# A dense block followed by sixteen streamed experts: the raw weights' pool is moved, and the first expert loads are put in another order

## The chip, the cores and the metric

One core of a Trainium2 chip runs the whole program. The metric is the device time of one execution in microseconds (us); what counts is the median over the runs. TensorE is called PE, VectorE DVE, ScalarE ACT, GpSimd POOL, and SyncE SP; SP issues most of the transfers.

## The reference, cut to what matters

A 512 x 1024 activation passes two mixer layers and then a second block: dense projections, three mixers, an output projection, a router, and a mixture of 16 experts in which each expert takes the 64 tokens that score highest for it.

```python
def second_block(...):
    ...
    mixed = jnp.concatenate([rms_norm_2(y_hy, ...), rms_norm_2(y_na, ...), rms_norm_2(y_pool, ...)], axis=-1)
    x = x + mixed @ w_out[i]
    x = x + expert_choice_moe(rms_norm_2(x, norm2_g[i]), w_router[i], w_gate[i], w_up[i], w_down[i])
    return rms_norm_2(x, final_g)

def expert_choice_moe(h, w_router, w_gate, w_up, w_down):
    cap = EC_CAPACITY * L // N_EXPERTS                    # 64 tokens
    aff = jax.nn.softmax(h @ w_router, axis=-1)
    gate, idx = lax.top_k(aff.transpose(0, 2, 1), cap)
    xs = jax.vmap(lambda hb, ib: hb[ib])(h, idx)
    a = jnp.einsum('becd,edf->becf', xs, w_gate)          # each expert: 3 matrices of 1024 x 2048, float32
    b = jnp.einsum('becd,edf->becf', xs, w_up)
    y = jnp.einsum('becf,efd->becd', jax.nn.silu(a) * b, w_down)
    ...
```

The weights of the experts are 16 x 3 x 8 MB = 402.7 MB of float32, and each byte is used once.

## The kernel before, in words

**Two stages.** The dense stage (both mixer layers, the second block's mixers and its output projection) runs first, out of pools that `build` opens one on top of the other in SBUF: `np` (norms and sums), `wp` (the dense weights), `xp` (the operands `xhi` and `xlo`, two buffers of 16 KB per partition each), and above these a pool that changes from mixer to mixer. A dense weight arrives raw (`wraw`, two buffers of 4 KB) and is split by ACT and DVE into `whi` and `wlo` (three buffers each); `group` multiplies them. The last four groups are the output projection: two that read the operand MA, one that reads MB, and one that reads `mn`. MA lies in an `xhi` buffer, MB in an `xlo` buffer, and `mn` in the other `xhi` buffer. In these four groups a PE row `acc<-xhi,wlo` is one of MA, `acc<-xlo,wlo` one of MB, and `acc<-mn,wlo` one of `mn`.

**The expert stage.** When the dense pools close, one pool of `moe_body` takes their room. An expert's weights come in 12 loads of 128 x 4096 float32 (2,097,152 bytes): four parts of the gate matrix (`mg`) and four of the up matrix (`mu`), in turns, then four of the down matrix (`md`); 192 loads in all. They land in nine places of 16 KB per partition, `w0` to `w8`, and for the first expert also in `ZH` and in the room of the activations `H` (called "t" in the code). `wtile` hands the places out: first in the order of the list `FIRST`, then round and round. Every load stands on SP's queue, in program order, by `load` and `preload`; SP issues one only after the waits of that load are over. A load's waits are those for whatever used the bytes of its place last.

**Where the places lie.** In KB from the start of a partition, by the built programs (the change moves only the dense side of this table):

| place | KB | dense tiles there, before | dense tiles there, after the change |
|---|---|---|---|
| ZH | 42.9 to 58.9 | norm temporaries, two `whi` | the same |
| w0 | 74.9 to 90.9 | `wraw`, half of the `mn` buffer | the `mn` buffer |
| w1 | 90.9 to 106.9 | half of `mn`, half of MA | MA |
| w2 | 106.9 to 122.9 | half of MA, half of MB | MB |
| w3 | 122.9 to 138.9 | half of MB, half of the other `xlo` | the other `xlo`, last read by the projections `qk0`, `qk1` |
| w4 | 138.9 to 154.9 | half of the other `xlo`, `YN` | `wraw`, `YN` |
| w5 to w8 | 154.9 to 218.9 | tiles of the mixers | the same |

**Between the stages** stands the router: PE computes the logits (`lg`) and the sums of squares (`nrm`), ACT copies the logits and takes the root, PE turns the logits (`lgT`), DVE and ACT make the softmax (`aff`), and `resid` transposes the activations (`xt`, copied to `res`). `rank` counts for each token of an expert how many score higher, and `gather` builds the expert's input. `idle` fills PE with matmuls whose result nobody reads.

**An expert.** `up` multiplies the gathered input with the `mg` and `mu` parts (64 matmuls each), `down` the result with the `md` parts (64); beside this `scatter` adds the expert before into the sum.

Of the kernel before, what the change touches and what calls it, by code (L numbers as in the profile page):

```python
# [19 lines left out]
S = 512  # L20
D = 1024
# [180 lines left out]
class Kern:  # L202
# [69 lines left out]
        if name in self.dbg:  # L272
            self.nc.gpsimd.dma_start(out=self.dbg[name], in_=ap)

    IDLE = 12, 2, 13


    WBUF = 3
# [16 lines left out]
    def fetch(self, w=None):  # L295
        if self.pos == len(self.seq):
            return
        nc = self.nc
        n, i, src = self.seq[self.pos]
        self.pos += 1  # L300
        if w is None:
            w = self.wp.tile([128, 2, 512], F32, name="wraw", bufs=2)
            (nc.gpsimd if n.startswith("wo") else nc.sync).dma_start(out=w, in_=src)
        hi = self.wp.tile([128, 2, 512], F32R, name="whi", bufs=self.WBUF)
        lo = self.wp.tile([128, 2, 512], F32R, name="wlo", bufs=self.WBUF)
        with self.tc.high_priority(1000):
# [110 lines left out]
    def pp_proj(self, l):  # L417

        nc = self.nc
        P = tuple(self.big.tile([128, 2, 512], F32R, name=n, bufs=1) for n in ("phi", "plo"))  # L420
        praw = self.wp.tile([128, 2, 512], F32, name="praw", tag="wraw", bufs=2)
        nc.scalar.dma_start(out=praw, in_=self.I["pT"][l])
        for k in range(2):
            self.split_x(P, k, praw[:, k, :])
        self.pp = self.big.tile([128, 8, 512], F32, name="pp", bufs=1)
        for half in range(2):
            wh, wl = self.take(f"pp{l}", half)
            for j in range(4):
                a = self.acc()
                c = slice(j * 128, j * 128 + 128)  # L430
                for k in range(2):
                    self.mm3(a, wh[:, k, c], wl[:, k, c], P[0][:, k, :], P[1][:, k, :], k == 0, k == 1)
                nc.scalar.activation(self.pp[:, half * 4 + j, :], a, AF.Copy)
# [35 lines left out]

    def X2(self):  # L470
        return tuple(self.xp.tile([128, 8, 512], F32R, name=n, bufs=2) for n in ("xhi", "xlo"))

    def open_dense(self):
        tc, ctx = self.tc, self.ctx
        self.np = ctx.enter_context(tc.tile_pool(name="np", bufs=1))
        self.wp = ctx.enter_context(tc.tile_pool(name="wp", bufs=1))
        self.xp = ctx.enter_context(tc.tile_pool(name="xp", bufs=1))

    def first(self, names):

# [908 lines left out]
    def mixout(self, M):  # L1389
# [23 lines left out]
            return t  # L1413

        def summed(t, first, last):
            for i in range(4):
                nc.tensor.matmul(nrm[:, i:i + 1], t[:, i * 128:i * 128 + 128], self.ones[:, :1], start=first and i == 0,
                                 stop=last and i == 3, skip_group_check=True)

        for g in range(2):  # L1420
            self.group(MA, f"wo{g}", "T", ev(g, False), steps=(3, 0))
# [17 lines left out]
        def ev1(j, a):  # L1439
            b = 4 + j  # L1440
            ev(1, False)(j, a)
            if b < 6:
                nc.gpsimd.tensor_add(sq, sq, square(b))
            else:
                S[b] = square(b)
            if b < 7:
                return lambda: self.logits(lg, b)

            def f():
                self.logits(lg, 7)  # L1450
                summed(sq, True, False)
                nc.vector.tensor_add(S[6], S[6], S[7])
                summed(S[6], False, True)
            return f

        self.group(M, "wo1", "T", ev1, (first4,), steps=(1, 2), apart=True)
# [9 lines left out]
    PARTS = 0, 2, 1, 3  # L1466


    FIRST = "w8", "w7", "w6", "w5", "w4", "w2", "w3", "ZH", "w0", "w1", "t"

    def moe_body(self, R, out, mp):
        nc, I = self.nc, self.I
# [10 lines left out]
        def wtile(keep=False):  # L1483

            n = (places or ring).pop(0)
            if n not in ring and n[0] == "w" and not keep:
                ring.append(n)
            if n == "t":
                return self.H.rearrange("p a c -> p (a c)")
            t = tile_(n)  # L1490
            if n == "ZH":
                early["ZH"] = t
            return t

        def load(e, i):


            n, i = SEQ[i]
            W[e, n, i] = w = wtile()
            src = I[n]  # L1500
            if e == 15 and i == (3 if n == "md" else self.PARTS[-1]):

                m = 1024 if n == "md" else 2048
                for k in range(0, 4096, m):
                    early["last"] = nc.sync.dma_start(out=w[:, k:k + m], in_=bass.AP(tensor=src.tensor, ap=[[4096, 128], [1, m]],
                                                      offset=src.offset + (e * 4 + i) * 128 * 4096 + k))
                return
            nc.sync.dma_start(out=w, in_=bass.AP(tensor=src.tensor, ap=[[4096, 128], [1, 4096]],
                                                 offset=src.offset + (e * 4 + i) * 128 * 4096))

        def preload(e, k0, k1):
            for i in range(k0, k1):
# [2 lines left out]
        def junk(name="junk"):  # L1515
# [1 line left out]


        tile_ = Tiles(mp, ss=(128, 3, 4), xt=(128, 8, 64, 2), oh=(128, 4, 64, 2), ZH=(128, 4096, 1), res=(128, 4, 1024, 1),
                      **{f"w{i}": (128, 4096, 1) for i in range(self.WB)}, rtok=(128, 4, 1), rs=(128, 4, 1), aff=(128, 4, 16, 1),  # L1520
                      mx=(128, 4, 1), cnt=(128, 3, 4, 2), rank=(128, 4, 3), fin=(128, 4, 4, 1), at=(128, 4, 2, 1), ai=(128, 1, 1), fl=(128, 4, 1))
        res = tile_("res")
        preload(0, 0, len(self.FIRST) - 1)
        lt = junk("lt")
        nc.scalar.activation(lt, lg, AF.Copy)
        r, mx, rs = tile_("rtok"), tile_("mx"), tile_("rs")
        nc.scalar.activation(rs, nrm[:, :4], AF.Sqrt, bias=self.eps, scale=1.0 / D)
        warm = tile_("ss")
        nc.scalar.activation(warm[:, 0:1], rs[:, 0:1], AF.Exp, scale=-1.0)
        V.reciprocal(r, rs)  # L1530
        aff = tile_("aff")
        p = self.tp("lgT")
        for i in range(4):
            routed = nc.tensor.matmul(p[:, i * 16:i * 16 + 16], lt[:, i * 128:i * 128 + 128], self.sel, start=i == 0, stop=i == 3,
                                      skip_group_check=True)
        p = p[:, :64].rearrange("p (i e) -> p i e", i=4)
        V.tensor_reduce(mx, p, AX.X, OP.max)
        V.tensor_sub(aff, p, mx[:, :, None].to_broadcast([128, 4, 16]))
# [77 lines left out]
        def up(e):  # L1616
# [5 lines left out]
            for at, (i, (n, A)) in enumerate(itertools.product(self.PARTS, (("mg", G), ("mu", U)))):  # L1622
                w = W.pop((e, n, i))
                for k in range(2):
                    for b in range(2):
                        for t in range(2):
                            c = k * 2048 + t * 1024 + b * 512
                            mm = nc.tensor.matmul(A[b][t * 64:t * 64 + 64, :], xt[:, 2 * i + k, :], w[:, c:c + 512],  # L1628
                                                  start=at < 2 and k == 0, stop=at > 5 and k == 1, skip_group_check=True)
                with self.tc.issue_after(mm.ins):  # L1630

                    if e and first <= at < first + 4:
                        scatter(e - 1, at - first)
# [103 lines left out]
        def resid(i):  # L1737
            for hf in range(2):
                q = self.acc("xt")
                for k in range(4):  # L1740
                    nc.tensor.transpose(q[:, k * 128:k * 128 + 128], h[:, hf * 4 + k, i * 128:i * 128 + 128], self.ident)
                nc.scalar.activation(res[:, i, hf * 512:hf * 512 + 512], q, AF.Copy)

        with self.tc.issue_after(routed.ins), self.tc.issue_after(ex.ins):
            resid(0)
            i = self.idle(self.IDLE[1])
        with self.tc.issue_after(i.ins):
            i = rank(0)
        with self.tc.issue_after(i.ins):
            for i in range(1, 4):  # L1750
                resid(i)
            self.idle(self.IDLE[2])
        gather(0)
        preload(0, len(self.FIRST) - 1, len(self.FIRST))
        total = None
        for e in range(15):
            preload(e, len(self.FIRST) if e == 0 else 0, NSEQ)
# [39 lines left out]
def build(ctx, tc, I, out, dbg=None):  # L1797
# [3 lines left out]
    def whole(fast):  # L1801
        with ExitStack() as es:
            K.np = es.enter_context(tc.tile_pool(name="np", bufs=1))
            K.wp = es.enter_context(tc.tile_pool(name="wp", bufs=1))
            K.xp = es.enter_context(tc.tile_pool(name="xp", bufs=1))
            X, sq = K.start(S_FOX + S_T0 + S_REC + S_T1 + S_SEC)
            A = K.fox(X, sq)
            K.h = K.H
# [31 lines left out]
```

## Time and profile before

| | us |
|---|---|
| median of 3 runs (1849.95 to 1851.24) | 1851.19 |
| the profiled execution | 1849.2 |
| its span, first to last instruction | 1847.0 |
| PE busy | 1792.5 |
| DVE busy | 839.7 |
| ACT busy | 495.7 |

The span has 2.2 us less than the profiled execution, which lie around it. PE is busy in 97% of the span, but the end of a matmul is modelled, so this share alone does not say that PE is at its limit. The transfers are half idle in the first half of the span, and from about the middle on they run at one rate without a break.

### The profile page before, as it was taken

Reading aid. Unit: us, or ns where it says so; the run is one execution under the profiler, and the core shown is the slowest. Engines: PE = TensorE matmul, PEld = TensorE weight load, DVE = VectorE, ACT = ScalarE, POOL = GpSimd, SP = SyncE. Lnnn points to the kernel's source line nnn. Section 1 sums busy time; section 2 is a strip of 40 time slices with the busy share of each in tenths; the row PEclk is TensorE's granted clock in tenths of the full one; section 3 lists DMA queues with packets and bytes.
Section 4 is the critical chain, followed back from the end, with each engine's and each line's share of the span. In section 5 each row is a group of like instructions: output and inputs, shape, how many; then the busy total and the mean of one; then the engine's idle time right before and its main releaser. Section 6 shows DMA issues by size and latency. Waiting matters only on the chain.

```text
span 1847.0 us, 21691 instructions
## 1 busy us (share of the span) xinstructions
PE 1792.5 (97%) x8654; PEld 1024.1 (55%) x8654; DVE 839.7 (45%) x1939; ACT 495.7 (27%) x863; POOL 21.8 (1%) x35
## 2 busy tenths in 40 slices
PE   9999999999999999999999999999999999999997
PEld 6767677888888888876743333333333333333332
DVE  6564767774644684678532223332223321333222
ACT  6453644463433464237401000000000000000011
POOL 0000000000000000000100000000000000000000
PEclk9999999999999999999999999999999999999999
DMA  5322233232221226434799999999999999999997
GB/s 168 114 81 86 75 118 128 101 99 95 65 80 57 96 88 219 132 117 172 286 403 403 421 426 428 427 428 427 428 427 428 427 427 428 428 427 429 427 427 323
DMA packets 57993, 497.18 MB, mean 269 GB/s; under 512 B 7017, under 2 KB 8169, under 8 KB 32667
## 3 DMA queue, kind: packets, MB, share of 16 engines
q1 hardware_dynamic: 48420, 470.46, 62.8%
q10 hardware_dynamic: 7592, 18.70, 3.1%
q0 software_dynamic: 1872, 6.55, 1.1%
q8 instruction: 70, 1.15, 0.2%
q14 instruction: 39, 0.32, 0.1%
HBM read 491.20 MB, written 4.49 MB: 268 GB/s over the span
## 4 chain that ended last, share of the span: by engine, by line
PE 75%; DMA 17%; DVE 5%; ACT 1%; issue 1%; ACTq 0%; POOLq 0%; SPq 0%; DVEq 0%
DMA w<-mu 11%; PE y L1675 11%; PE acc L339 11%; PE acc L340 11%; PE acc L341 10%; PE u L1628 8%; PE g L1628 7%; PE gx L1580 3%; PE st L1734 2%; DMA w<-mg 2%; DMA w<-md 2%; DMA wraw<-wg 1%; PE hT L1662 1%; PE pt L639 1%; PE sc L335 1%
## 5 line engine op out<-in xcount | busy, mean ns | idle before, releaser
L339 PE MATMUL acc<-xhi,whi 128*128 128x512 f32 x800 | 317.5, 399 | 0.9 <-ACT xhi L325 0.8
L341 PE MATMUL acc<-xhi,wlo 128*128 128x512 f32 x800 | 313.8, 393 | 0.0
L340 PE MATMUL acc<-xlo,whi 128*128 128x512 f32 x784 | 307.6, 392 | 0.2 <-DVE xlo L326 0.2
L1735 DVE TENSOR_TENSOR H<-H,st 128x512 f32<-128x512 f32 x120 | 78.1, 683 | 489.1 <-PE st L1734 489.1
L1628 PE MATMUL g<-w,xt 128*64 128x512 f32 x1024 | 260.2, 595 | 10.7 <-DMA w<-mg 10.6
L1628 PE MATMUL u<-w,xt 128*64 128x512 f32 x1008 | 248.0, 596 | 7.3 <-DMA w<-mu 6.9
L308 DVE TENSOR_TENSOR wlo<-wraw,whi 128x1024 fp32r<-128x1024 f32 x127 | 155.1, 1222 | 185.7 <-ACT whi L307 167.9
L1675 PE MATMUL y<-w,ZH 128*64 128x512 f32 x1008 | 237.0, 595 | 0.6 <-DMA w<-md 0.6
L307 ACT ACTIVATE whi<-wraw 128x1024 fp32r<-128x1024 f32 x127 | 134.3, 1057 | 214.1 <-PE acc L340 135.5
L339 PEld LDWEIGHTS acc<-xhi,whi 128*128 128x128 f32 x800 | 150.5, 188 | 37.8 <-issue 3.6
L1628 PEld LDWEIGHTS g<-w,xt 128*64 128x64 f32 x1024 | 79.5, 137 | 163.5 <-issue 135.6
L341 PEld LDWEIGHTS acc<-xhi,wlo 128*128 128x128 f32 x800 | 150.3, 188 | 30.9 <-issue 0.7
L340 PEld LDWEIGHTS acc<-xlo,whi 128*128 128x128 f32 x784 | 147.4, 188 | 32.2 <-issue 3.1
L1628 PEld LDWEIGHTS u<-w,xt 128*64 128x64 f32 x1008 | 76.3, 137 | 148.0 <-issue 126.7
L1675 PEld LDWEIGHTS y<-w,ZH 128*64 128x64 f32 x1008 | 73.9, 137 | 140.0 <-issue 136.6
L1648 ACT ACTIVATE gs<-g 128x512 f32<-128x512 f32 x32 | 19.1, 597 | 402.6 <-PE g L1628 386.3
L1580 PE MATMUL gx<-res,oh 128*64 128x256 f32 x512 | 62.3, 385 | 10.8 <-DVE H L1735 10.8
L1734 PE MATMUL st<-ZH 64*128 64x512 f32 x240 | 67.7, 641 | 0.0
L1612 ACT ACTIVATE ZH<-ogT 128x512 f32<-128x512 f32 x15 | 9.0, 597 | 207.1 <-PE ogT L1610 207.1
L339 PE MATMUL acc<-whi,xhi 128*128 128x512 f32 x160 | 64.3, 403 | 0.0
L341 PE MATMUL acc<-whi,xlo 128*128 128x512 f32 x160 | 62.9, 393 | 0.0
L340 PE MATMUL acc<-wlo,xhi 128*128 128x512 f32 x160 | 62.9, 393 | 0.0
(528 smaller groups left out, 1896.6 us busy)
## 6 DMA issues: line engine op xcount, KB each, us to landing
w<-mg SPq DMA_DIRECT2D x63, 2048.0 KB, 32.2
w<-mu SPq DMA_DIRECT2D x62, 2048.0 KB, 31.2
w<-md SPq DMA_DIRECT2D x62, 2048.0 KB, 34.7
wraw<-wg SPq DMA_DIRECT2D x115, 512.0 KB, 3.5
cb<-cd ACTq DMA_DIRECT2D x16, 256.0 KB, 3.5
wraw<-wg POOLq DMA_DIRECT2D x8, 512.0 KB, 3.8
nab<-nab ACTq DMA_DIRECT2D x12, 256.0 KB, 2.7
H<-xT SPq DMA_DIRECT2D x8, 256.0 KB, 5.5
```

The lines of the kernel that those rows point to most:

```text
L307: self.last = nc.scalar.activation(hi, w, AF.Copy)
L308: nc.vector.tensor_sub(lo, w, hi.bitcast(F32))
L335: mm(*a, skip_group_check=True, **k)
L339: mm(out, wh, xh, start=start, stop=False)
L340: mm(out, wh, xl, start=False, stop=False)
L341: mm(out, wl, xh, start=False, stop=stop)
L1580: nc.tensor.matmul(Q[w][t * 64:t * 64 + 64, :256], oh[:, i, :], rv[:, i, t, w], start=i == 0, stop=i == 3, skip_group_check=True)
L1628: mm = nc.tensor.matmul(A[b][t * 64:t * 64 + 64, :], xt[:, 2 * i + k, :], w[:, c:c + 512], start=at < 2 and k == 0, stop=at > 5 and k == 1 ...
L1648: nc.scalar.activation(g, G[b], AF.Silu)
L1675: nc.tensor.matmul(Y[t * 64:t * 64 + 64, :], hT[:, i % 2 * 4 + k, i // 2, :], w[:, k, t * 512:t * 512 + 512], start=kk == 0 and e < 15, st ...
L1734: nc.tensor.matmul(q, OHT[e][sl, i * 128:i * 128 + 128], YY[e][sl, :], start=True, stop=True)
L1735: V.tensor_add(total[:, i, t * 512:t * 512 + 512], total[:, i, t * 512:t * 512 + 512], q)
```

## The change

- The raw dense weights leave `wp` for a pool of their own, `wr`, which is opened above `xp`. The operand buffers thereby come to lie 8 KB lower, each of them on exactly one place (table above).
- `FIRST`, the order in which the places are handed out, and `ORDER`, the order in which the first ten loads are issued, are new: the first load goes to `w2`. The twelfth load, the last `md` part of the first expert, goes into `w2` again, in two halves, and it and what follows are now recorded after the first part of the first expert's matmuls.
- In the router the sums of squares are made with `ones` as the other operand (12 matmuls of 32 x 128 in place of 8 of 128 x 1; a sum on DVE goes away), the root is taken over 128 x 128 and turned by PE afterwards, the copy of the logits is shared by DVE and ACT, two idle matmuls stand earlier, half of the residual's transposes stand ahead of `rank`, and the last run of idle matmuls has 9 in place of 13.

```diff
-    IDLE = 12, 2, 13
+    IDLE = 12, 2, 9
...
-            w = self.wp.tile([128, 2, 512], F32, name="wraw", bufs=2)
+            w = self.wr_.tile([128, 2, 512], F32, name="wraw", bufs=2)
...
         def summed(t, first, last):
             for i in range(4):
-                nc.tensor.matmul(nrm[:, i:i + 1], t[:, i * 128:i * 128 + 128], self.ones[:, :1], start=first and i == 0,
-                                 stop=last and i == 3, skip_group_check=True)
+                m = nc.tensor.matmul(nrm[32 * i:32 * i + 32, :128], self.ones[:, :32], t[:, i * 128:i * 128 + 128], start=first,
+                                     stop=last, skip_group_check=True)
+            return m
...
-                nc.vector.tensor_add(S[6], S[6], S[7])
-                summed(S[6], False, True)
+                summed(S[6], False, False)
+                m = summed(S[7], False, True)
+                with self.tc.issue_after(m.ins):
+                    self.idle(self.IDLE[1])
...
-    FIRST = "w8", "w7", "w6", "w5", "w4", "w2", "w3", "ZH", "w0", "w1", "t"
+    FIRST = "w2", "w8", "w7", "w6", "w5", "w1", "w3", "w4", "ZH", "w0", "t"
+
+    ORDER = 0, 1, 2, 3, 4, 5, 6, 8, 7, 9
...
+            if early.get(n):
+                t, early[n] = early[n], None
+                return t
             t = tile_(n)
+            if n == self.FIRST[0] and n not in early:
+                early[n] = t
...
+                m = 2048 if (e, i, n) == (0, len(self.FIRST) - 8, "md") else 4096
+            for k in range(0, 4096, m):
+                early["last"] = nc.sync.dma_start(out=w[:, k:k + m], in_=bass.AP(tensor=src.tensor, ap=[[4096, 128], [1, m]],
+                                                  offset=src.offset + (e * 4 + i) * 128 * 4096 + k))
...
-        preload(0, 0, len(self.FIRST) - 1)
-        lt = junk("lt")
-        nc.scalar.activation(lt, lg, AF.Copy)
+        for i in self.ORDER:
+            load(0, i)
+        lt, rt = junk("lt"), junk("rt")
+        V.tensor_copy(lt[:, :256], lg[:, :256])
+        half = nc.scalar.activation(lt[:, 256:], lg[:, 256:], AF.Copy)
...
+            if i == 3:
+                nc.tensor.transpose(q[:, :128], rt[:, :128], self.ident)
...
+                if e + at == 0:
+                    preload(0, len(self.FIRST), NSEQ)
...
             resid(0)
-            i = self.idle(self.IDLE[1])
+            i = resid(1)
...
             K.xp = es.enter_context(tc.tile_pool(name="xp", bufs=1))
+
+            K.wr_ = es.enter_context(tc.tile_pool(name="wr", bufs=1))
```

SP's queue where the dense stage's last weight load is past, before (place, source, shape, and the engines whose progress the row itself waits for; a wait that an earlier row has made is not repeated):

```order
L1508 DMA w8_7435<-mg 128x4096 [waits DMAHW0_49,DMAHW1_49,DVE_49,PE_49]
L1508 DMA w7_7434<-mu 128x4096 [waits DMAHW1_49,DVE_49,PE_49]
L1508 DMA w6_7433<-mg 128x4096 [waits DMAHW4_49,DMAHW5_49,DMAHW3_49,DMAHW6_49,DMAHW2_49,DMAHW7_49,DVE_49,PE_49]
L1508 DMA w5_7432<-mu 128x4096 [waits PE_49,DVE_49,Activation_49,Pool_49]
L1508 DMA w4_7431<-mg 128x4096 [waits DVE_49]
L1508 DMA w2_7429<-mu 128x4096 [waits PE_49]
L1508 DMA w3_7430<-mg 128x4096
```

The same rows of SP's queue in the changed program:

```order
L1515 DMA w2_7439<-mg 128x4096 [waits DMAHW0_49,DVE_49,PE_49]
L1515 DMA w8_7445<-mu 128x4096 [waits DMAHW1_49]
L1515 DMA w7_7444<-mg 128x4096 [waits DMAHW2_49]
L1515 DMA w6_7443<-mu 128x4096 [waits DMAHW6_49,DMAHW5_49,DMAHW7_49,DMAHW4_49,DMAHW3_49]
L1515 DMA w5_7442<-mg 128x4096 [waits Pool_49]
L1515 DMA w1_7438<-mu 128x4096
L1515 DMA w3_7440<-mg 128x4096
L1515 DMA w4_7441<-md 128x4096 [waits DMASW4_49,DMASW3_49,DMASW5_49,DMASW2_49,DMASW6_49,DMASW1_49,DMASW7_49,DMASW0_49,DVE_49]
```

The load into `w2` has moved from the sixth row to the first, and its wait for PE with it. That wait is for the same matmul in both programs: the last one that reads MB. None of the seven rows behind it waits for PE on its own account any more, since the first row's wait is later in PE's order than any of theirs.

PE's router before, from the last logits to the first expert's ranking (`bc` is in `rank`):

```order
L1387 MATMUL lg<-H,wr 32x512 x4
L1417 MATMUL nrm<-ones,sqx_7095 128x1 x4
L1417 MATMUL nrm<-ones,sqx 128x1 x4
L1534 MATMUL lgT<-sel,lt 128x16 x4
L1741 MATMUL xt<-ident,H 128x128 x8
L268 LDWEIGHTS identb
L268 MATMUL idle<-identb 128x512
...
L1550 MATMUL bc<-ident,aff 128x128 x4
L1741 MATMUL xt<-ident,H 128x128 x24
```

The same stretch of PE's queue in the changed program:

```order
L1381 MATMUL lg<-H,wr 32x512 x4
L1412 MATMUL nrm<-sqx_7098,ones 32x128 x4
L1412 MATMUL nrm<-sqx,ones 32x128 x8
L268 LDWEIGHTS identb
L268 MATMUL idle<-identb 128x512
...
L1545 MATMUL lgT<-sel,lt 128x16 x4
L1755 MATMUL xt<-ident,H 128x128
L1544 MATMUL rootT<-ident,rt 128x128
L1755 MATMUL xt<-ident,H 128x128 x15
L1562 MATMUL bc<-ident,aff 128x128 x4
L1755 MATMUL xt<-ident,H 128x128 x16
```

The two idle matmuls have moved ahead of `lgT`, eight of the residual's transposes have moved ahead of `bc`, and the transpose of the root is new. Everything on PE ahead of this stretch stands in the same order in both programs.

## Rows read from the trace of the kernel before

**Rows 1.** The page's head, and its forty slices of the transfers.
```profile
span 1847.0 us, 21691 instructions
...
DMA  5322233232221226434799999999999999999997
GB/s 168 114 81 86 75 118 128 101 99 95 65 80 57 96 88 219 132 117 172 286 403 403 421 426 428 427 428 427 428 427 428 427 427 428 428 427 429 427 427 323
```
**Rows 2.** Windows: stretch, length, busy PE PEld DVE ACT POOL, PEclk, DMA, GB/s.
```profile
823.00:901.00 78.00, 77.22 (x462) 57.11 (x462) 58.17 (x173) 48.78 (x112) 3.16 (x6) 1.00 0.54 197
901.00:1100.00 199.00, 196.15 (x975) 81.61 (x976) 59.99 (x193) 24.14 (x38) 6.45 (x5) 0.99 0.97 407
1100.00:1350.00 250.00, 244.40 (x1170) 87.15 (x1166) 76.10 (x230) 10.75 (x18) 0.00 (x0) 1.00 1.01 427
1350.00:1800.00 450.00, 423.07 (x1998) 150.75 (x1996) 120.40 (x352) 23.62 (x40) 0.00 (x0) 1.00 1.01 427
```
**Rows 3.** Waits of PE, 1350 to 1847 us: us in total, times, longest.
```profile
PE g L1628 <- DMA w<-mg: 10.6, 11, 1.3
PE u L1628 <- DMA w<-mu: 6.9, 8, 1.2
...
PE y L1675 <- DMA w<-md: 0.6, 1, 0.6
```
**Rows 4.** Chain that ended last: ends of experts 0 and 2, expert 1's last part.
```profile
981.80 0.42 PE y L1675
...
1010.32 3.58 PE u L1628 x16
...
1092.71 0.42 PE y L1675
```
**Rows 5.** Timeline of SP, 820 to 936 us: start, length of the issue, operation.
```profile
823.97 0.33 SPq L1508 DMA_DIRECT2D w<-mg  x1
855.04 0.33 SPq L1508 DMA_DIRECT2D w<-mu  x1
869.16 0.33 SPq L1508 DMA_DIRECT2D w<-mg  x1
877.71 0.33 SPq L1508 DMA_DIRECT2D w<-mu  x1
895.09 0.33 SPq L1508 DMA_DIRECT2D w<-mg  x1
901.03 0.33 SPq L1508 DMA_DIRECT2D w<-mu  x1
```
**Rows 6.** Waits of SP, 820 to 1000 us: us in total, times, longest.
```profile
SPq L1508 <- PE acc L341: 5.6, 1, 5.6
```
**Rows 7.** Transfers issued 890 to 898 us: KB, us from issue to landing.
```profile
w<-mg SPq DMA_DIRECT2D x1, 2048.0 KB, 7.8
```
**Rows 8.** Timeline of PE, 840 to 912 us, single rows.
```profile
845.98 0.40 PE L340 MATMUL acc<-xlo,whi 128*128 128x512 f32 x1
...
889.73 0.39 PE L341 MATMUL acc<-xhi,wlo 128*128 128x512 f32 x1
...
900.61 0.39 PE L341 MATMUL acc<-xlo,wlo 128*128 128x512 f32 x1
900.84 0.39 PE L339 MATMUL acc<-mn,whi 128*128 128x512 f32 x1
```
**Rows 9.** Timeline of PE in the router, 914 to 936 us, three rows.
```profile
914.90 1.95 PE L1417 MATMUL nrm<-ones,sqx 128*128 128x1 f32 x16
...
923.65 2.97 PE L268 MATMUL idle<-identb 128*128 128x512 bf16 x13
...
930.70 1.02 PE L1628 MATMUL g<-w,xt 128*64 128x512 f32 x2
```
**Rows 10.** Windows, the ten us in which PE's clock is lowest.
```profile
910.00:920.00 10.00, 10.00 (x56) 7.31 (x55) 4.50 (x15) 5.72 (x11) 2.58 (x2) 0.87 0.83 329
```
**Rows 11.** Timeline of PE at the end of the span, the last two `md` parts.
```profile
1829.68 7.09 PE L1675 MATMUL y<-w,ZH 128*64 128x512 f32 x32 [0.58 <-DMA w<-md]
```

More of the change, by code (lines that the diff above doesn't have):

```diff
@@ L420, in pp_proj @@
         P = tuple(self.big.tile([128, 2, 512], F32R, name=n, bufs=1) for n in ("phi", "plo"))
-        praw = self.wp.tile([128, 2, 512], F32, name="praw", tag="wraw", bufs=2)
+        praw = self.wr_.tile([128, 2, 512], F32, name="praw", tag="wraw", bufs=2)
         nc.scalar.dma_start(out=praw, in_=self.I["pT"][l])
@@ L471, in X2 @@
         return tuple(self.xp.tile([128, 8, 512], F32R, name=n, bufs=2) for n in ("xhi", "xlo"))
[L473 to L477, printed above, removed]
     def first(self, names):
@@ L1503, in load @@
                 m = 1024 if n == "md" else 2048
[L1504 to L1509, printed above, removed]
+            else:
+                m = 2048 if (e, i, n) == (0, len(self.FIRST) - 8, "md") else 4096
+            for k in range(0, 4096, m):
+                early["last"] = nc.sync.dma_start(out=w[:, k:k + m], in_=bass.AP(tensor=src.tensor, ap=[[4096, 128], [1, m]],
+                                                  offset=src.offset + (e * 4 + i) * 128 * 4096 + k))
         def preload(e, k0, k1):
@@ L1519, in moe_body @@
         tile_ = Tiles(mp, ss=(128, 3, 4), xt=(128, 8, 64, 2), oh=(128, 4, 64, 2), ZH=(128, 4096, 1), res=(128, 4, 1024, 1),
-                      **{f"w{i}": (128, 4096, 1) for i in range(self.WB)}, rtok=(128, 4, 1), rs=(128, 4, 1), aff=(128, 4, 16, 1),
+                      **{f"w{i}": (128, 4096, 1) for i in range(self.WB)}, rtok=(128, 4, 1), aff=(128, 4, 16, 1),
                       mx=(128, 4, 1), cnt=(128, 3, 4, 2), rank=(128, 4, 3), fin=(128, 4, 4, 1), at=(128, 4, 2, 1), ai=(128, 1, 1), fl=(128, 4, 1))
         res = tile_("res")
-        preload(0, 0, len(self.FIRST) - 1)
-        lt = junk("lt")
-        nc.scalar.activation(lt, lg, AF.Copy)
[L1526 to L1530, printed above, removed]
+        for i in self.ORDER:
[3 more added lines that the diff above has]
+        half = nc.scalar.activation(lt[:, 256:], lg[:, 256:], AF.Copy)
+        r, mx = tile_("rtok"), tile_("mx")
+        with self.tc.issue_after(half.ins):
+            nc.scalar.activation(rt[:, :128], nrm[:, :128], AF.Sqrt, bias=self.eps, scale=1.0 / D)
+            warm = tile_("ss")
+            nc.scalar.activation(warm[:, 0:1], rt[:, 0:1], AF.Exp, scale=-1.0)
         aff = tile_("aff")
-        p = self.tp("lgT")
+        p, q = self.tp("lgT"), self.av("rootT")
         for i in range(4):
+            if i == 3:
+                nc.tensor.transpose(q[:, :128], rt[:, :128], self.ident)
             routed = nc.tensor.matmul(p[:, i * 16:i * 16 + 16], lt[:, i * 128:i * 128 + 128], self.sel, start=i == 0, stop=i == 3,
                                       skip_group_check=True)
+        V.reciprocal(r, q[:, 0:128:32])
         p = p[:, :64].rearrange("p (i e) -> p i e", i=4)
@@ L1740, in resid @@
                 for k in range(4):
-                    nc.tensor.transpose(q[:, k * 128:k * 128 + 128], h[:, hf * 4 + k, i * 128:i * 128 + 128], self.ident)
+                    t = nc.tensor.transpose(q[:, k * 128:k * 128 + 128], h[:, hf * 4 + k, i * 128:i * 128 + 128], self.ident)
                 nc.scalar.activation(res[:, i, hf * 512:hf * 512 + 512], q, AF.Copy)
+            return t
         with self.tc.issue_after(routed.ins), self.tc.issue_after(ex.ins):
             resid(0)
-            i = self.idle(self.IDLE[1])
+            i = resid(1)
         with self.tc.issue_after(i.ins):
@@ L1749, in moe_body @@
         with self.tc.issue_after(i.ins):
-            for i in range(1, 4):
+            for i in range(2, 4):
                 resid(i)
@@ L1756, in moe_body @@
         for e in range(15):
-            preload(e, len(self.FIRST) if e == 0 else 0, NSEQ)
+            if e:
+                preload(e, 0, NSEQ)
             if e == 13:
```

## The prediction

> **What bounds the kernel now.** I read the forty slices of the page first. From the twentieth slice on the transfers are busy in every slice and move 403 to 429 GB/s, while in the slices ahead they are mostly idle [rows 1]. The table by stages says the same with sharper ends: 427 GB/s and a full DMA share from 1100 to 1800 us [rows 2]. One load is 2.097152 MB, so at 427 GB/s it takes 2.097152 / 0.427 = 4.911 us, and an expert of twelve loads takes 58.9 us. PE alone is a little quicker: from the end of expert 0 to the end of expert 2 the chain counts 1092.71 - 981.80 = 110.9 us, 55.5 us for an expert [rows 4]. So PE, which begins with a stock of loads, gains 3.5 us on the transfers with each expert until the stock is gone. The waits of PE show where that is: none is named for a weight between 1100 and 1350 us (that view has only waits for DVE), and after 1350 us there are 11 waits for `mg` and 8 for `mu` [rows 3]. The last `md` matmuls start on the arrival of their weights too, after a wait of 0.58 us [rows 11]. From there to the end nothing of the change is found. Hence the stream of 192 loads sets the end: **what moves the end is when the stream starts and how much it idles before it is full**, and a microsecond gained by PE in the router is worth nothing by itself.
>
> **The start of the stream.** Five loads are issued before 901 us, one by one, as the places come free: 823.97, 855.04, 869.16, 877.71, 895.09 [rows 5]. The fifth lands 7.8 us after its issue [rows 7], at 902.9 us. The sixth, into `w2`, is issued at 901.03 [rows 5] after a wait of 5.6 us for a PE matmul of line 341 [rows 6]. It is the last that reads MB: it starts at 900.61 and the next row already reads `mn` [rows 8].
>
> **The changed order on SP.** In the changed program the load into `w2` stands first on SP's queue, and it waits for that same matmul, since `w2` now lies on MB alone. PE's order ahead of it is unchanged and PE is busy in 77.22 of the 78 us before it [rows 2], so it cannot come noticeably earlier; I take 901.03 us again. SP issues in order. The loads into `w8`, `w7`, `w6` and `w5`, whose places are free at 824 to 878 us as before, stand behind the waiting row, and so do those into `w1` (MA, last read at 889.73 [rows 8]) and `w3`. Who waits for that is the stream: the transfers do nothing for the experts before 901 us.
>
> What this costs, counted at the fifth load. Before it lands at 902.9. Now the first load lands at 901.03 + 7.8 = 908.8 and the fifth four loads later, at 908.8 + 4 x 4.911 = 928.5. The stream is behind by **25.6 us**.
>
> **What comes back.** Before, the stream is not full after 901 us: the stretch to 1100 us moves 407 GB/s in place of 427 [rows 2], which is 199 x (427 - 407) / 427 = 9.3 us of idle transfers, lost where a load waits for its place. Now eight loads are free to go at 901 us, and they alone keep the transfers busy to 901.03 + 2.9 + 8 x 4.911 = 943 us (the 2.9 is what the single load's 7.8 has beyond 4.911). `ZH` waits for the last of the sums of squares and `w0` for the last `mn` matmul; both are over when PE adds those sums up, from 914.90 us [rows 9]. The first load that needs anything of expert 0 is the twelfth, the halves of `w2`. Its turn comes at 908.8 + 10 x 4.911 = 957.9 us, and expert 0 begins on PE at 930.70 [rows 9], 27 us earlier. So no place makes the stream wait any more, and the 9.3 us are regained whole. I take all of it; the bounds are nothing and 9.3.
>
> Does PE then run dry early? The twentieth load, the last that expert 1's up half needs, lands at 908.8 + 19 x 4.911 = 1002.1 us, and PE comes to it at 1010.32 [rows 4], a margin of 8.2 us. With each expert the same load comes 58.9 us later and PE wants it 55.5 us later, so the margin is 4.8, 1.4 and then below nothing: in expert 4, at 1010.3 + 3 x 55.5 = 1177 us. From there PE waits for weights, where before it first did so after 1350 us. It loses nothing by that but its lead, since the end hangs on the last load either way.
>
> **The halves.** The twelfth load in two pieces can start after half a part of matmuls. But the queue is full by then, so it is worth nothing. The Trainium skill says in "Perfetto Trace Analysis", DMA Optimizations, that splitting transfers may let some start sooner; by that rule half a part, some 1.8 us of the 3.58 that a part takes [rows 4], would come off the sum, but the rule is given for idle transfers, and here they are not.
>
> **The router.** From the sums of squares at 914.90 to the first `g` at 930.70 is 15.8 us of PE's time [rows 9]. Four idle matmuls fewer save 4 x 2.97 / 13 = 0.9 us; twelve sums in place of eight add at most half of 1.95 us; a transpose is added; a sum on DVE and half of ACT's copy go, neither of which I put above the 1.95 us of the sums. PE's clock shows 0.87 on average in 910 to 920 us, a stretch at 1.2 in place of 2.4 GHz [rows 10]; the two idle matmuls now stand where it falls, which may give back up to 10 x 0.13 = 1.3 us. All this lies between -4 and +1.5 us for expert 0's start, and I take -2. It is covered by the 27 us above on one side and by the loads on the other: **nothing** of it reaches the end. The cover would have to lose 27 us before it cost anything. The pool `wr` itself moves addresses and no work: nothing.
>
> **The sum**, against the profiled execution: 1849.2 + 25.6 - 9.3 = 1865.5 us. That execution is 2.0 us below the median of the runs, 1851.19; the same +16.3 on the median gives 1867.5. I take **1867.0** for the median after.
>
> **Rivals.**
> *The idle is not regained.* If the loads behind the eighth still find their places late, up to 9.3 us more stay: 1849.2 + 25.6 = 1874.8, or 1877 on the median. Against it speak the 27 us at the twelfth load. Chance 0.08, above the range or at its top.
>
> *PE is the bound.* If the end hung on PE's chain, the late loads would be hidden by the stock and the router's 2 us would count: about 1849, within 0.2%. PE's busy share of 97% speaks for it; the 19 waits for `mg` and `mu` [rows 3] and the equal 427 GB/s before and after 1350 us speak against it. Chance 0.03.
>
> *The place is free much earlier (faster).* If the tile under `w2` were not MB but the other `xlo` buffer, last read at 845.98 [rows 8], the row would hold nobody up: `w2`, `w8` at 846, `w7`, `w6`, `w5` as before, `w1` at 890, `w3` behind it, `w4` at about 898. By 901 us the stream would be two loads further than now, 9.8 us, and the time 1849.2 - 9.8 = 1839.4, 1841 on the median. With everything behind it, the release decides: the shift is the release - 901.03 + 16.3, which is zero for a release at 884.7 us, and the kernel would be faster below that. The row that waits is the same in both programs, which leaves little room. Chance 0.04. That the change doesn't do what it says is this case turned round: the list is not in the order of release, since `w3`'s and `w1`'s places are free before `w2`'s.
>
> *A lower rate.* The rows hold 427 GB/s over 700 us [rows 2]. The Trainium skill, "DMA: Bandwidth & Descriptors", Where 436 GB/s comes from, gives about 358 GB/s as what binds a core's loads from memory. By it a load would take 5.86 us, an estimate, the fifth would come 29.4 us later, nothing would be regained, and the time would be 1878.6. The measurement differs and decides: no chance.
>
> **How the numbers follow.** The forecast has 0.85, and its own spread comes from the landing (7.8 us in one row), from the regained idle, and from the distance of profiled run and median: 1861 to 1873, which with a part of the first rival is the range. About 0.2%, 3.7 us, is what a measurement of this kernel can tell from no change. Faster 0.04, within it 0.03, slower 0.85 + 0.08 = 0.93.
>
> **What would show it.** No load of `mg`, `mu` or `md` on SP before 900 us, and then seven or eight within 5 us; a DMA share of 1.00 in every ten us from 910 on; first waits of PE for `mg` or `mu` at about 1177 us in place of after 1350; expert 0 starting on PE at 928 to 931 us; a span of about 1863. It is wrong if loads stand in SP's timeline before 885 us, or if the transfers idle again between 930 and 1080 us.

## The result and the profile after

The changed kernel is slower, as forecast: 1867.85 us in the median of 4 runs (1865.38 to 1870.19), against 1850.57 (1847.43 to 1851.24, 4 runs) for the kernel before. The ratio on record is 1.0097 with a 95% interval of 1.0085 to 1.0109; it is not the ratio of the two medians, which lie 17.3 us apart. A difference of +16.3 us had been forecast. The profiled execution took 1868.7 us, its span 1866.5.

The page of the changed kernel, its head and the forty slices of the transfers (the same rows as [rows 1]):

```profile
span 1866.5 us, 21697 instructions
...
DMA  4322233222121326312699999999999999999997
GB/s 166 114 80 85 74 125 122 101 95 100 57 80 57 105 99 227 110 66 86 260 426 428 427 429 426 428 428 427 429 427 427 428 426 428 428 427 428 427 427 326
```

The eighteenth and nineteenth slices moved 117 and 172 GB/s before and move 66 and 86 now: the stream of expert weights starts later. From the twenty-first slice on there is no slice below 426 but the last, where before three were at 403, 403 and 421.

The windows of the changed kernel (stretch, length, busy PE PEld DVE ACT POOL, PEclk, DMA share, GB/s), to be set beside [rows 2]; the second fence has the forty us after 900 in tens:

```profile
823.00:901.00 78.00, 77.22 (x469) 57.12 (x466) 58.28 (x181) 50.04 (x112) 3.17 (x6) 1.00 0.21 68
901.00:1100.00 199.00, 194.34 (x986) 81.28 (x987) 62.00 (x197) 23.80 (x38) 6.45 (x5) 1.00 0.98 416
1100.00:1350.00 250.00, 232.19 (x1098) 81.78 (x1095) 64.17 (x192) 9.55 (x16) 0.00 (x0) 1.00 1.01 428
1350.00:1800.00 450.00, 421.56 (x1996) 148.50 (x1998) 128.53 (x384) 20.77 (x35) 0.00 (x0) 1.00 1.01 427
```

```profile
900.00:910.00 10.00, 10.00 (x49) 8.02 (x47) 6.20 (x9) 2.62 (x5) 2.20 (x2) 1.00 0.44 156
910.00:920.00 10.00, 10.00 (x72) 6.40 (x71) 3.27 (x8) 3.48 (x7) 4.25 (x4) 1.00 1.01 430
920.00:930.00 10.00, 8.17 (x65) 6.19 (x66) 7.32 (x36) 5.44 (x11) 0.00 (x0) 1.00 1.01 433
930.00:940.00 10.00, 10.00 (x56) 4.11 (x54) 1.70 (x4) 1.28 (x1) 0.00 (x0) 1.00 1.00 426
```

The timeline of SP from 820 us (start, length of the issue, operation), which answers [rows 5], and SP's waits from 820 to 1000 us (us in total, times, longest), which answer [rows 6]:

```profile
904.64 0.33 SPq L1515 DMA_DIRECT2D w<-mg  x1
905.02 0.42 SPq L1515 DMA_DIRECT2D w<-mu  x1
905.49 0.42 SPq L1515 DMA_DIRECT2D w<-mg  x1
906.09 0.71 SPq L1515 DMA_DIRECT2D w<-mu  x1
906.85 0.51 SPq L1515 DMA_DIRECT2D w<-mg  x1
907.40 0.49 SPq L1515 DMA_DIRECT2D w<-mu  x1
907.93 0.46 SPq L1515 DMA_DIRECT2D w<-mg  x1
908.71 0.33 SPq L1515 DMA_DIRECT2D w<-md  x1
```

```profile
SPq L1515 <- DVE xlo L326: 86.4, 1, 86.4
SPq L1515 <- PE acc L341: 19.9, 1, 19.9
```

No load goes out before 904.64 us, and then eight go out within 4.1 us. That is a queue behind one waiting row. The two wait rows belong to the same row of the queue: it first waits for DVE to finish writing a tile, then 19.9 us for the last PE matmul that reads MB; before, the load into `w2` waited 5.6 us for it, and five loads had gone out ahead. The Trainium skill says in "DMA: Bandwidth & Descriptors", in the section on the anatomy of one DMA (SWDGE path), that a semaphore wait is made on the issuing sequencer ahead of dispatch while the DMA engines only consume their queues; the trace agrees: of the seven loads behind the first, six are for places (also called rooms below) that the rows before have free at 824 to 890 us, and all leave after it.

### The profile page after: what moved, and what is told of

It reads as the page before. It is cut to its first block, busy times and chain, and to the rows that moved or that the text cites. A ratio compares the mean times of both kernels' runs of the same rounds, so it can differ in the third digit from the quotient of the medians.

```text
span 1866.5 us, 21697 instructions
## 1 busy us (share of the span) xinstructions
PE 1794.1 (96%) x8659; PEld 1020.7 (55%) x8659; DVE 839.8 (45%) x1939; ACT 495.4 (27%) x863; POOL 21.4 (1%) x35
## 4 chain that ended last, share of the span: by engine, by line
PE 66%; DMA 26%; DVE 5%; ACT 1%; issue 1%; POOLq 0%; SPq 0%; ACTq 0%; DVEq 0%
DMA w<-mu 18%; PE acc L339 11%; PE acc L340 11%; PE acc L341 11%; PE y L1689 10%; PE u L1640 5%; DMA w<-mg 4%; PE gx L1592 3%; PE g L1640 3%; DMA w<-md 2%; PE st L1748 1%; DMA wraw<-wg 1%; PE hT L1676 1%; PE pt L633 1%; PE sc L335 1%
## 5 line engine op out<-in xcount | busy, mean ns | idle before, releaser
L1640 PE MATMUL g<-w,xt 128*64 128x512 f32 x1024 | 252.3, 596 | 15.5 <-DMA w<-mg 15.4
L1640 PE MATMUL u<-w,xt 128*64 128x512 f32 x1008 | 244.7, 597 | 16.3 <-DMA w<-mu 15.6
```

## The experiments

All of them edit one of the two kernels, most in one line; none leaves out any of the computation. The load that is issued first is called the head below.

**The list in the order of release.** The pool, the halves and the router stay, only `FIRST` changes:

```diff
-    FIRST = "w2", "w8", "w7", "w6", "w5", "w1", "w3", "w4", "ZH", "w0", "t"
+    FIRST = "w8", "w3", "w7", "w6", "w5", "w1", "w4", "w2", "ZH", "w0", "t"
```

> The changed kernel with its list in the order in which the places really come free: w8, w3, w7, w6, w5, w1, w4, w2, ZH, w0, t. Theory (the stream of loads sets the end, and its start is held by the row that waits for MB): loads stand on SP from 824 us on again, and the loss goes. How much beyond it? If only the start of the stream counts, two loads more than before are in by 905 us, and the time is 1850.6 - 9.8 = 1841. If the number of places caps the lead (all eleven rooms are full by 932 us, and the twelfth load waits for expert 0's first matmuls, the nineteenth for its first down part), the lead is lost there and only the router's 1.5 to 2 us of earlier start and a little more stay: 1846 to 1849. Rival (the router or PE is what made the change slower): stays near 1867.

Measured: 1847.05 us (1846.08 to 1849.29, 11 runs) against 1849.78 for the kernel before on that chip, ratio 0.9988 (0.9979 to 0.9997). The whole loss is gone, and the gain that is left, 2.7 us, is under a third of the 9.8 that an earlier start alone would bring.

SP's timeline and the windows of this kernel show both halves of that:

```profile
823.44 0.33 SPq L1515 DMA_DIRECT2D w<-mg  x1
845.74 0.33 SPq L1515 DMA_DIRECT2D w<-mu  x1
854.38 0.33 SPq L1515 DMA_DIRECT2D w<-mg  x1
...
920.79 0.33 SPq L1515 DMA_DIRECT2D H<-md  x1
931.82 2.04 SPq L1515 DMA_DIRECT2D w<-md  x2
```

```profile
823.00:901.00 78.00, 77.21 (x462) 57.04 (x461) 58.82 (x174) 48.77 (x110) 3.17 (x6) 1.00 0.64 239
901.00:1100.00 199.00, 194.33 (x988) 79.10 (x988) 58.96 (x192) 23.17 (x37) 6.44 (x5) 1.00 0.95 395
```

```profile
910.00:920.00 10.00, 9.89 (x86) 7.45 (x85) 4.91 (x18) 6.78 (x14) 2.58 (x2) 1.00 0.64 246
920.00:930.00 10.00, 8.28 (x56) 4.49 (x56) 6.12 (x30) 2.32 (x5) 0.00 (x0) 1.00 0.91 385
930.00:940.00 10.00, 10.00 (x48) 3.36 (x48) 0.39 (x1) 0.47 (x1) 0.00 (x0) 1.00 0.69 244
```

Up to 901 us it moves 239 GB/s where the kernel before moved 197 [rows 2], which puts the stream 78 x (239 - 197) / 427 = 7.7 us ahead. Then the rooms run out. The eleventh load goes out at 920.79, and the twelfth has to wait until 931.82, when expert 0's first matmuls have read a part; the transfers idle meanwhile. From 901 to 1100 us 199 x (427 - 395) / 427 = 14.9 us are idle, against 9.3 before, so 5.6 of the 7.7 us are given back.

**Only the order, in the old layout.** The kernel before with `w2` moved to the head of its own list, no other edit:

```diff
-    FIRST = "w8", "w7", "w6", "w5", "w4", "w2", "w3", "ZH", "w0", "w1", "t"
+    FIRST = "w2", "w8", "w7", "w6", "w5", "w4", "w3", "ZH", "w0", "w1", "t"
```

> The kernel before with one line changed: its list begins with w2 (w2, w8, w7, w6, w5, w4, w3, ZH, w0, w1, t). The old layout, the old router, no halves. In the old layout w2 lies half on MA and half on MB, so its load waits for the same matmul. The stream theory expects the whole loss from this one line: +16 to +20, 1867 to 1870. Rival (pool, halves or router are to blame): 1850.6.

Measured: 1865.59 us (1865.22 to 1866.35, 4 runs), ratio 1.0087 (1.0072 to 1.0103). Moving one name costs 15.8 us, all but 1.5 of what the whole change costs. This is a little under the +16 to +20 expected. The head goes out at 901.27 us:

```profile
901.27 0.33 SPq L1508 DMA_DIRECT2D w<-mg  x1
```

**Another room at the head.** The changed kernel with `w1`, which lies on MA, ahead of all others, and with `w0`, which lies on the buffer of `mn`:

```diff
-    FIRST = "w2", "w8", "w7", "w6", "w5", "w1", "w3", "w4", "ZH", "w0", "t"
+    FIRST = "w1", "w8", "w7", "w6", "w5", "w3", "w4", "w2", "ZH", "w0", "t"
```

> The changed kernel with w1 in the place of w2 at the head of the list (w1, w8, w7, w6, w5, w3, w4, w2, ZH, w0, t). Its first load waits for the last matmul that reads MA, at 890 us in the trace of before, in place of 901. The stream theory's formula, shift = release - 884.7, gives +5.3: 1856. A theory in which the cost comes from the layout or the router gives 1867 as in the changed kernel.

Measured: 1854.86 us (1854.01 to 1858.89, 5 runs), ratio 1.0035 (1.0021 to 1.0048): +5.1 us on the medians, and 890.80 - 884.7 = 6.1 by the formula with the head that its trace has:

```profile
890.80 0.33 SPq L1515 DMA_DIRECT2D w<-mg  x1
```

```diff
-    FIRST = "w2", "w8", "w7", "w6", "w5", "w1", "w3", "w4", "ZH", "w0", "t"
+    FIRST = "w0", "w8", "w7", "w6", "w5", "w3", "w1", "w4", "ZH", "w2", "t"
```

> The changed kernel with w0 in place of w2 at the head of the list of first loads (w2 goes where w0 stood), nothing else. The last reader of the room that w0 is laid over was done at about 913 us in the changed kernel's trace (916.9 to 918.2 is where its load into w0 went out, behind ZH), 8.7 to 12 us later than w2's. By the theory that the head's release sets the end one for one (release less 884.7): a release of 913 to 915 gives +28 to +30 on the kernel before, 1878 to 1880 us. By the rival that the transfers regain part of so late a start from the idle time behind it: no more than about 1872, and some idle time left between 920 and 1100.

Measured: 1876.49 us (1875.67 to 1878.95, 4 runs) against 1849.91, ratio 1.0147 (1.0132 to 1.0163): +26.6 us with a head released at 912.45:

```profile
912.45 0.33 SPq L1515 DMA_DIRECT2D w<-mg  x1
```

It is 1.5 us under the range that the theory gave. About half a us of this is the release, which came ahead of the 913 assumed: 912.45 - 884.7 = 27.8. The rest is no more than the interval of the ratio leaves open. Nothing was regained from the idle time behind the head, since there is none: the windows show 428 GB/s from 920 to 1100 us.

**The old router behind the late head.** The changed kernel's pool, halves and list, with the router of the kernel before (the main lines of the edit):

```diff
-    IDLE = 12, 2, 9
+    IDLE = 12, 2, 13
...
-                m = nc.tensor.matmul(nrm[32 * i:32 * i + 32, :128], self.ones[:, :32], t[:, i * 128:i * 128 + 128], start=first,
-                                     stop=last, skip_group_check=True)
-            return m
+                nc.tensor.matmul(nrm[:, i:i + 1], t[:, i * 128:i * 128 + 128], self.ones[:, :1], start=first and i == 0,
+                                 stop=last and i == 3, skip_group_check=True)
...
-            i = resid(1)
+            i = self.idle(self.IDLE[1])
```

> The changed kernel with the router as before (one root of 128 x 4, idle matmuls 2 and 13 where they were): pool, list, order and halves are those of the change. By the stream theory the router is covered: within 2 us of the changed kernel, 1866 to 1870. Rival (PE's start of expert 0 counts): 1.5 to 2 us more than the changed kernel.

Measured: 1866.14 us (1865.79 to 1867.57, 4 runs), ratio 1.0088 (1.0073 to 1.0104); with the new router it is 1.0097 (1.0085 to 1.0109). Expert 0 starts on PE at 935.16 us here, 2.5 us later than in the changed kernel, and the end does not move. It differs from the kernel before with `w2` at the head in the pool, the halves and the rest of the list, and has the same ratio, 1.0088 against 1.0087, so neither the pool nor the halves are seen in the end, to within the 3 us that either interval reaches to each side.

**The router where the head is not late.** Both ways: the list in order of release with the old router, and the kernel before with the new one. The edits are those just shown, and for the first the list of the first experiment.

> The changed kernel's pool and halves, the first loads in the order of their rooms' release, and the router of the kernel before. With this list the rooms are all taken by about 932 us and the next load waits for expert 0's first matmuls, so what the router costs PE ahead of expert 0 (1.5 us more from the last sums to the first g in the old code) should come through to the end: 1.5 to 2 us slower than the same list with the new router (1847.05), that is 1848.5 to 1849. By the rival that the router is covered here as it was behind the late load: no difference, 1847.0.

Measured: 1849.51 us (1847.43 to 1853.33, 11 runs) against 1849.91, ratio 1.0001 (0.9992 to 1.0010); 0.5 us above the range expected.

> The kernel before with the router's edits alone (transposes ahead, squares in quarters), old pools and old list. In the kernel before the twelfth load waits for expert 0's first matmuls, as with the list in order of release. If PE's earlier start of expert 0 comes through: 1.5 to 2 us faster, 1847.8 to 1848.3 with the kernel before at 1849.8. If the router is covered by the stream: no difference.

Measured: 1847.75 us (1845.21 to 1851.42, 11 runs), ratio 0.9991 (0.9982 to 1.0000).

With the list in order of release the new router is worth 0.13% (1.0001 against 0.9988), 2.4 us; in the kernel before it is worth 0.09%, 1.7 us, whose interval just touches no change. The difference of the first two ratios, each known to 0.09%, is itself known to about 0.13%, so that neither figure alone is clear of nothing; they agree with each other, and with the 1.5 us that PE's rows show below. Where PE decides, the edit is thus worth about 2 us; behind the late head no gain is seen.

**The halves.** The list in order of release, with the twelfth load whole. (The text below calls it the load into "t"; the load into "t" is the eleventh, and it is whole in all the kernels.)

```diff
-                m = 2048 if (e, i, n) == (0, len(self.FIRST) - 8, "md") else 4096
+                m = 4096
```

> The first loads in the order of their rooms' release, new router, and the load into t whole in place of two halves. If the halves are worth nothing: 1847.0, as with them. If the half that is laid over the earlier room starts ahead to a gain, the whole load goes out later by up to the distance of the two releases, and while the queue has nothing else to move that is up to 2 us: at most 1849.

Measured: 1848.80 us (1846.22 to 1852.01, 11 runs), ratio 0.9992 (0.9983 to 1.0001), against 0.9988 with halves. The difference of 0.04% is smaller than the 0.09% that either interval reaches to each side: nothing that can be told from none, and up to 3 us are not excluded. The traces narrow it. Whole, the load goes out 5.07 us after expert 0's start:

```profile
935.57 0.33 SPq L1515 DMA_DIRECT2D w<-md  x1
```

In halves the first goes out 3.35 us after it, so half a load starts 1.7 us sooner; the load behind it goes out 8.50 us after expert 0's start in both. By these rows the halves can bring the stream forward by 1.7 us at most.

**How much PE may be late.** 55 more idle matmuls ahead of expert 0 are 10 us of PE, 149 more are 30:

```diff
-    IDLE = 12, 2, 9
+    IDLE = 12, 2, 64
```

> The changed kernel with 55 more idle matmuls on PE ahead of expert 0's gather (nothing reads them), so that expert 0's first matmul starts 10 us later. In the traces so far the span was the release of the head of the list plus 961.6 us, or, where that is less, expert 0's first matmul plus about 916. In the changed kernel the first is 17.6 us above the second (904.64 + 961.6 against 932.68 + 916), so by this theory 10 us on PE cost nothing: 1866 to 1869 us. By the rival that PE's start of expert 0 counts beside the stream: 1878.

Measured: 1865.35 us (1864.72 to 1866.62, 4 runs) against 1851.06, ratio 1.0084 (1.0067 to 1.0101). Ten us on PE cost nothing; the time is even 0.65 us under the range expected, with a head at 900.41.

```diff
-    IDLE = 12, 2, 9
+    IDLE = 12, 2, 158
```

> The same with 149 more idle matmuls, 30 us. By the theory of the later of two chains the cover is 17.6 us and the rest comes through: +12.4, 1880 us. By the prediction's cover of 27 us only 3 would come through: 1871. If PE counts in full: 1898.

Measured: 1879.99 us (1878.14 to 1881.39, 4 runs), ratio 1.0159 (1.0142 to 1.0175). Of 30 us 12 to 15 come through. The chain of waits of this kernel has the idle matmuls in it, and two of its windows show where the transfers then run dry:

```profile
923.37 34.10 PE idle L268 x158
```

```profile
950.00:960.00 10.00, 10.00 (x59) 4.84 (x57) 0.42 (x1) 0.00 (x0) 0.00 (x0) 1.00 0.87 367
960.00:970.00 10.00, 10.00 (x50) 3.90 (x50) 1.27 (x3) 1.28 (x1) 0.00 (x0) 1.00 0.41 148
```

The third of these runs puts the 10 us into the list in order of release:

> First loads in the order of their rooms' release, with the 55 more idle matmuls ahead of expert 0. Here the chain that runs through expert 0's start sets the end by the theory (the twelfth load waits for its first matmuls), so the 10 us come through whole: 1847 + 10 = 1857 us. By the rival that the stream covers PE here too: 1847 to 1849.

Measured: 1858.43 us (1855.91 to 1859.12, 5 runs), ratio 1.0039 (1.0025 to 1.0053), where without the delay it is 0.9988: 0.51%, 9.4 us of the 10.

**All profiled executions in one table.** "Head" is the issue of the first expert load, "e0" the start of expert 0's first `g` matmul, both from the timelines; the last two columns are differences.

| kernel | head | e0 | span | span - head | span - e0 |
|---|---|---|---|---|---|
| changed | 904.64 | 932.68 | 1866.5 | **961.9** | 933.8 |
| old router behind the late head | 903.92 | 935.16 | 1865.4 | **961.5** | 930.2 |
| before, `w2` at the head | 901.27 | 931.23 | 1863.0 | **961.7** | 931.8 |
| `w1` at the head | 890.80 | 929.76 | 1852.7 | **961.9** | 922.9 |
| `w0` at the head | 912.45 | 928.39 | 1873.5 | **961.1** | 945.1 |
| changed, e0 10 us later | 900.41 | 938.52 | 1862.8 | **962.4** | 924.3 |
| changed, e0 30 us later | 903.09 | 961.50 | 1878.8 | 975.7 | **917.3** |
| before | 823.97 | 930.70 | 1847.0 | 1023.0 | **916.3** |
| before with the new router | 823.56 | 928.45 | 1845.6 | 1022.0 | **917.2** |
| order of release | 823.44 | 928.47 | 1843.8 | 1020.4 | **915.3** |
| the same, old router | 825.46 | 932.09 | 1847.4 | 1021.9 | **915.3** |
| the same, no halves | 825.42 | 930.50 | 1846.6 | 1021.2 | **916.1** |
| the same, e0 10 us later | 824.72 | 939.77 | 1856.8 | 1032.1 | **917.0** |

Six kernels end 961.1 to 962.4 us after their head, wherever PE stands; seven end 915.3 to 917.3 us after expert 0's start, wherever their stream begins. The span is the later of two chains: a full stream from a late head, or a stream that has taken all eleven rooms and then follows PE from expert 0's first part on. With 961.6, the mean of the five late heads without a delay, and the 916.3 of the kernel before, they cross where the head is released 961.6 - 916.3 = 45.3 us ahead of e0; with the kernel before's e0 of 930.7 that is at 885.4 us.

## Why the prediction was right

**The stream sets the end: right.** Six kernels with heads from 890.80 to 912.45 us, 21.7 us apart, have the same distance from head to end within 1.3 us. The windows hold 427 to 428 GB/s from 1100 to 1800 us in both kernels. The rival *PE is the bound* is out: 10 us more on PE cost nothing in the changed kernel. So is the *lower rate*: neither window from 1100 to 1800 us is under 427 GB/s. The Trainium skill's page "HBM Reference", Specifications (TRN2), gives about 425 GB/s for a core that streams alone, and 358 for each of two that stream at once. This program runs on one core, and its trace agrees with the first, at 427.

**The queue behind `w2`: right, by the edit alone.** Moving that one name in the kernel before gives +15.8 us. The release of 901.03 us was taken over from the profile before; the kernel before with `w2` at the head has 901.27. The changed kernel's profiled execution has 904.64, and the four other kernels with `w2` at the head lie between 900.41 and 903.92. The changed kernel and its two versions with a late expert 0 are the same program up to the head, and they have 904.64, 900.41 and 903.09. So this is a spread between executions, and it arises in the dense stage. The chain of waits has it in a row there, first of the changed kernel, then of the kernel before, then of the list in order of release:

```profile
816.11 4.32 PE yh L1337 x20
```

```profile
812.47 4.32 PE yh L1343 x20
```

```profile
811.82 4.32 PE yh L1337 x20
```

The same row is 3.6 us later than before in one kernel with the new pool and 0.7 earlier in another, so the pool is not its cause; the cause stays open. The prediction's own rule takes it up: 904.64 - 884.7 = +19.9 us, and the two profiled executions differ by 1868.7 - 1849.2 = 19.5. That the median came within 1 us of the 1867.0 forecast is in part luck, since the head alone varies by 4.2 us over these five kernels.

**The idle time regained whole: right.** Every ten us from 910 to 1100 is full, at 423 to 433 GB/s, and the rival in which the 9.3 us stay does not happen. The term -9.3 and the term +25.6 were each worked out from one row, and their sum, +16.3, is between the +15.8 and +17.3 measured.

**The cover of 27 us: mis-sized.** The prediction said that PE's start of expert 0 could slip 27 us before it cost anything; by the table the two chains of the changed kernel stand 904.64 + 961.6 - (932.68 + 916.3) = 17.3 us apart, and 30 us of delay cost 12 to 15. The failing step is that it compared the twelfth load's turn, 957.9 us, with expert 0's start. The load goes out only when a part of matmuls has read its room (964.85 us in the kernel with 30 us of delay, 3.4 after e0), it needs time from issue to landing, and later loads wait on PE in the same way. In the changed kernel the twelfth load's turn, worked out as the prediction did but from the head at 904.64, is 28.9 us behind expert 0's start. Of the 11.6 us that are missing from it, reading the part takes 936.02 - 932.68 = 3.3 and landing 7.8 - 4.9 = 2.9; the other 5.4 go by this estimate to the later loads, which were not measured apart. In the kernel with 30 us of delay SP waits for `g` matmuls 13 times from 900 to 1100 us (us in total, times, longest).

```profile
SPq L1515 <- PE g L1640: 75.3, 13, 38.3
```

For the forecast it made no difference, since the change moves e0 by 2 us.

**The router: right on both sides.** From the last sums at 918.38 us to the first `g` at 932.68 it is 14.3 us, 15.8 before [rows 9]; the runs give 1.7 to 2.4 us where PE decides, near the 2 taken, though neither figure is larger than its own uncertainty, and nothing that is seen behind the late head. Rows of the changed kernel's PE timeline:

```profile
918.38 0.82 PE L1412 MATMUL nrm<-sqx,ones 128*32 128x128 f32 x12
919.12 0.60 PE L268 MATMUL idle<-identb 128*128 128x512 bf16 x2
...
932.68 1.02 PE L1640 MATMUL g<-w,xt 128*64 128x512 f32 x2
```

**The halves: right for the changed kernel as far as rows go.** The transfers are full at 936 us, where they are issued. Where they are not full, the difference could not be told from none either.

**When PE runs dry: one expert off.** PE first waits for a weight at 1109.87 and 1125.45 us, in expert 3, where 1177 us, in expert 4, had been forecast; PE's timeline of the changed kernel:

```profile
1109.87 3.65 PE L1640 MATMUL g<-w,xt 128*64 128x512 f32 x16 [1.05 <-DMA w<-mg]
```

The margins 8.2, 4.8, 1.4 start 1.6 lower, as the head is 3.6 us later and e0 only 2.0: 6.6, 3.2 and then below nothing. The step was sound, but the margin left at the third expert was smaller than the spread of the release that it hung on.

**The rival on the faster side: mis-sized.** For an early release it gave -9.8 us, the full lead at 901 us. The list in order of release has most of that lead there (7.7 us by the windows) and ends 2.7 us ahead. The step that failed is "With everything behind it, the release decides", carried on below its own break-even: below about 885 us it is no longer the release that decides but expert 0's start, since there are eleven rooms and the twelfth load waits for PE. The prediction had used just this to explain the 9.3 us of idle time in the kernel before, and left it out of the rival. Its break-even, 884.7 us, is where the two chains cross (885.4 by the table), so it was right as the point from which the change costs, and wrong as the point from which it pays.

**A version that beats both.** The list in order of release, with the changed pool and router, is 0.12% under the kernel before (0.9988, 0.9979 to 0.9997) and 1.1% under the changed kernel. Most of it is the router: with the old router the same list is at 1.0001.

## What to carry to other kernels

A list of transfers on one queue is an order of waits: sort it by the time at which each destination comes free, since a row that waits longest holds back every row whose place is free already. Here the loss came from one late place put first; sorting the rest as well brought nothing over the kernel before (1.0001 with the same router). Before a gain is counted from an earlier start, ask which of two chains ends later, the stream from its first transfer or the stream from the point where the buffers are all taken; an edit can be worth 2 us on one side of that crossing and nothing on the other, and a delay test of 10 us tells on which side a kernel stands.

## What the runs showed of the hardware

**PE's clock.** In all four profiled kernels with the old router the granted clock fell in the router: 0.87 in 910 to 920 us before [rows 10] and 0.96 in the ten us behind it, and 0.66 in one ten us of the kernel with the old router behind the late head, the worst case. None of the nine with the new router shows less than 1.00 from 900 to 930 us. The worst case, first what PE did ahead of it, then its windows of 2 us:

```profile
917.75 1.95 PE L1417 MATMUL nrm<-ones,sqx 128*128 128x1 f32 x16
919.56 1.51 PE L1544 MATMUL lgT<-sel,lt 128*128 128x16 f32 x8
```

```profile
918.00:920.00 2.00, 2.00 (x20) 2.00 (x20) 0.21 (x4) 0.72 (x2) 0.00 (x0) 0.99 0.97 418
920.00:922.00 2.00, 2.00 (x11) 2.00 (x11) 0.85 (x4) 1.60 (x4) 0.00 (x0) 0.50 1.02 434
922.00:924.00 2.00, 2.00 (x10) 1.47 (x9) 0.80 (x4) 1.23 (x3) 0.00 (x0) 0.50 1.03 442
924.00:926.00 2.00, 2.00 (x11) 2.00 (x10) 1.36 (x5) 0.55 (x1) 0.00 (x0) 0.50 0.98 418
926.00:928.00 2.00, 2.00 (x17) 2.00 (x16) 1.93 (x11) 1.59 (x4) 0.00 (x0) 0.80 0.98 418
```

PE counts as busy throughout, and yet the clock stands at 1.2 GHz from 920 to 926 us, behind matmuls of 128x1 and 128x16. In the new router the sums have 128x128 and two idle matmuls of 128x512 follow at once. Which of the two keeps the clock was not tried apart.

**A starved PE that costs nothing.** With `w0` at the head PE waits 6.43 us for a weight of expert 0, and the clock is 0.74 in the ten us that follow:

```profile
961.19 5.61 PE L1640 MATMUL u<-ZH,xt 128*64 128x512 f32 x16 [6.43 <-DMA ZH<-mu]
```

```profile
960.00:970.00 10.00, 8.81 (x44) 3.73 (x46) 3.04 (x8) 0.00 (x0) 0.00 (x0) 0.74 0.99 422
```

Sixteen matmuls take 5.61 us there in place of 3.58, and the span is still 961.1 us from the head: behind a full stream even a wait of this size and a slow clock are covered.
